# The triangle for the forget gates' running sums: one VectorE instruction per layer in the place of a load

## The chip, the core and the metric

The kernel runs on one core of a Trainium2 chip. The metric is device time in microseconds (us) of one execution of the program on that core; the figure for a kernel is the median of its runs. PE is TensorE (its weight loads have a row of their own, PEld), DVE is VectorE, ACT is ScalarE, POOL is GpSimd, SP is SyncE, whose queue issues all transfers of this kernel.

## What is computed

Two layers of a trunk over 1040 rows (16 learned rows and 1024 of input) of width 1024. In each layer the rows are normalized and projected; one half of the columns feeds four heads of differential attention, the other half eight heads of forgetting attention, whose scores carry a running sum of log forget gates. Gates, an output projection and the residual follow. What touches the change:

```python
    log_f = jax.nn.log_sigmoid(ff.astype(jnp.float32) + forget_bias[l].astype(jnp.float32))
    cum_logf = jnp.transpose(jnp.cumsum(log_f, axis=1), (0, 2, 1))
    ...
    # forgetting_attention, one block of queries
    s = jnp.einsum('bhqd,bhkd->bhqk', qb, k).astype(jnp.float32) * scale
    s = s + cq[..., None] - cum_logf[:, :, None, :]
    visible = positions[None, :] <= pq[:, None]
    s = jnp.where(visible, s, -jnp.inf)
```

## The kernel before

The 1040 rows are cut into nine blocks (80 rows, seven times 128, 64) and these into three chunks `c` of three blocks. Each layer is a weave of two streams, written by hand into one order for PE: the attention of eight pairs of heads (scores `sc`, transposes `tp`, products with the values `po`; all products are recorded at L181, transposes at L185), and the fill, which is the projections that the next pair needs (`k`, `q`, `v` and gate units; products `pj`). A model clock in the Python code decides at build time how the two are woven; PE then runs its list strictly in that order. On the other engines the order is set by a scheduler at build time, and each engine runs its list in order too.

The weights of a unit come as four loads of 128 KB into `wst` (four buffers, L254, on SP's queue) and are split into `whi` (ACT L261 or POOL L263) and `wlo` (POOL or DVE, L265).

The third value unit of a layer (`v_unit`, u = 2) also makes the eight columns of forget gates, collected in the tile `ffz` (called `z` in the code), 72 columns: nine blocks of eight heads. `log_forget` (L540 on) turns them into log forget gates by a chain on DVE with one exponential on ACT: L544, L546, L549 to L561. Its working tiles are three of the ring `tc`, which has three buffers in all. The last instruction, L561, writes `ffz`.

`cumulate` is a function that `log_forget` returns; it is called a little later in the stream. It takes a fourth tile `upper` from the ring `tc` (so the buffer of the first of the three working tiles, whose last reader is L559), loads the upper triangle of ones into it from the table `cst` in main memory (L566, 128 x 128 float32, 64 KB), and lets PE form the sums of each block over its rows, nine float32 products of the triangle with a block of `ffz` (18 instructions in the trace). L577 on DVE adds the sum of the block before, L579 writes the result to the scratch `cscr`, and L823 loads it from there for each head, spread over all partitions. The forgetting heads need it for their scores.

Two more tables lie on chip from the start of the program, in bfloat16, in one tile `cb16`: `identb`, the identity, and `trib`, 1e30 strictly above the diagonal and 0 elsewhere. The scores of the forgetting heads use both as a mask (L652). In the order of instructions below this tile is printed as `cb_67`; the `cb` without that number are tiles of the ring `cb`.

Of the kernel before, what the change touches and what calls it, by code (L numbers as in the profile page):

```python
# [13 lines left out]
ALU = mybir.AluOpType  # L14

P = 128
# [51 lines left out]
C_ID, C_U, C_DM, C_DM0 = 0, 128, 256, 256 + T  # L68
# [18 lines left out]
def trunk_kernel(ctx, tc, x, meta, norm_gain, w_in, fbias, lq1, lk1, lq2, lk2,  # L87
                 subln, w_out, fgain, cst, cstb, rope, out):
    nc = tc.nc
# [7 lines left out]
    dma = nc.sync.dma_start  # L97
# [4 lines left out]
    identb, trib = cb16[:, 0:P], cb16[:, P:2 * P]  # L102
# [25 lines left out]
    def st(tag, w, dt=F32, bufs=None):  # L128
        bufs = bufs or {"tc": TCB}.get(tag, 3)
        return sb.tile([P, w], dt, name=tag, tag=tag, bufs=bufs)  # L130

    def big(tag, bufs, dt=F32):
        return sb.tile([P, T], dt, name=tag, tag=tag, bufs=bufs)
# [45 lines left out]
    def mm(o, a, b, start, stop, passes=1):  # L179
        n = b.shape[-1]  # L180
        nc.tensor.matmul(o, a, b, start=start, stop=stop)  # L181
        pe.add(b.dtype == BF16, max(n * passes * COL, 0.056))
# [29 lines left out]
    def proj_ps(tag="pj"):  # L212
        return ps.tile([P, 512], F32, name=tag, tag=tag, bufs={"pj": 2, "sc": SB, "tp": TB}[tag])
# [326 lines left out]
    def log_forget(l, z, box):  # L540

        n = NB * 8
        az = st("tc", CW)[:, :n]
        nc.vector.scalar_tensor_tensor(az, z, -1.0, z, ALU.mult, ALU.max)  # L544
        e = st("tc", CW)[:, :n]
        nc.scalar.activation(e, az, AF.Exp, scale=-1.0)  # L546

        d = st("tc", CW)[:, :n]
        nc.vector.tensor_scalar(d, e, 2.0, None, ALU.add)  # L549
        nc.vector.reciprocal(d, d)  # L550
        s = az
        nc.vector.tensor_tensor(s, e, d, ALU.mult)
        w = d
        nc.vector.tensor_tensor(w, s, s, ALU.mult)
        q = e
        nc.vector.tensor_scalar(q, w, 1.0 / 15, None, ALU.mult)
        for i in (13, 11, 9, 7, 5, 3):
            nc.vector.scalar_tensor_tensor(q, q, 1.0 / i, w, ALU.add, ALU.mult)
        nc.vector.scalar_tensor_tensor(q, q, 1.0, s, ALU.add, ALU.mult)  # L559
        nc.vector.tensor_scalar(z, z, 0.0, None, ALU.min)  # L560
        nc.vector.scalar_tensor_tensor(z, q, -2.0, z, ALU.mult, ALU.add)  # L561

        def cumulate():
            crow = big("cb", 2)
            upper = st("tc", CW)
            dma(out=upper[:, 0:P], in_=cst[:, C_U:C_U + P])  # L566
            for c in range(3):
                pt = proj_ps("sc")
                for j in range(3 * c, 3 * c + 3):
                    sz = BE[j] - BS[j]  # L570
                    o = BS[j] - CS[c]
                    mm(pt[:8, o:o + sz], z[:sz, j * 8:(j + 1) * 8], upper[:sz, :sz], True, True, 4)
                for j in range(3 * c, 3 * c + 3):
                    o = BS[j] - CS[c]
                    sz = BE[j] - BS[j]
                    prev = crow[:8, BS[j] - 1:BS[j]] if j else zero1[:8, :]
                    nc.vector.tensor_scalar(crow[:8, BS[j]:BE[j]], pt[:8, o:o + sz], prev, None,  # L577
                                            ALU.add)
            dma(out=cscr[l], in_=crow[:8, :])  # L579
            box["cum"] = True  # L580
            when["cum"] = pe.t + LCUM
        return cumulate
# [631 lines left out]
```

## Time and profile before

| | |
|---|---|
| median of 3 runs | 1623.01 us |
| the runs | 1619.45 to 1624.98 us |
| the profiled execution, its own time | 1622.79 us |
| its span, first to last instruction | 1620.9 us |
| PE busy | 1486.1 us, 92% of the span |
| DVE busy | 1056.3 us, 65% |
| ACT busy | 829.6 us, 51% |
| POOL busy | 688.5 us, 42% |
| mean granted clock of PE | 0.964 |

Time stamps count from the first instruction of the profiled execution. "Busy" is the time in which an engine has an instruction under way; on PE matmuls overlap, so busy does not mean full speed. The granted clock is a share of 2.4 GHz: 1.00 is 2.4 GHz, 0.50 is 1.2 GHz. In a row of a timeline the brackets hold the idle time before the instruction and what ended it. A share of busy time is an average over stages; what a change in one place is worth is read from that place.

### The profile page before, as it was taken

What the parts mean: (1) busy time and instruction counts of PE and PEld (TensorE: products, weight loads), DVE (VectorE), ACT (ScalarE), POOL (GpSimd) and SP (SyncE); (2) the same over time, 40 slices, a digit from 0 to 9 for tenths busy, and PEclk for the clock granted to TensorE, in tenths of its full rate; (3) what the DMA queues carried; (4) which work ended last, traced back from release to release, by engine and by line L of the source; (5) the groups of instructions that cost most, each with busy time, mean ns of one, the idle gap of its engine ahead of it and who ended that gap; (6) DMA issues with size and microseconds to landing.
All of it is one profiled execution on the core that took longest, in us unless ns stands there. A gap on an engine that the chain in (4) does not pass through costs nothing.

```text
span 1620.9 us, 30144 instructions
## 1 busy us (share of the span) xinstructions
PE 1486.1 (92%) x9932; PEld 1419.7 (88%) x9932; DVE 1056.3 (65%) x3024; ACT 829.6 (51%) x2067; POOL 688.5 (42%) x1125
## 2 busy tenths in 40 slices
PE   6988999978999999987998999999599999996897
PEld 5988999977999999887988898999599999995897
DVE  6588867864756565666655986596556555657554
ACT  6455556533655565543334655565256555655543
POOL 3453423312444344456756243240244442443664
PEclk9999999998999999988999999999799999998999
DMA  9342313202232323464434242131222232334554
GB/s 240 86 100 60 97 46 63 60 19 71 69 68 63 103 58 99 151 184 133 146 78 104 62 96 73 33 75 28 64 58 67 58 93 57 92 114 143 151 148 137
DMA packets 181469, 147.86 MB, mean 91 GB/s; under 512 B 19624, under 2 KB 176864, under 8 KB 181312
## 3 DMA queue, kind: packets, MB, share of 16 engines
q1 hardware_dynamic: 181312, 145.93, 33.9%
q8 instruction: 79, 1.29, 0.3%
q14 instruction: 78, 0.64, 0.1%
HBM read 117.49 MB, written 28.38 MB: 90 GB/s over the span
## 4 chain that ended last, share of the span: by engine, by line
PE 57%; DVE 11%; DMA 8%; issue 6%; POOL 3%; ACT 2%; SPq 0%; DVEq 0%; POOLq 0%; ACTq 0%
PE pj L181 36%; PE sc L181 8%; PE po L181 7%; PE tp L185 6%; DMA wst<-in_w_out_dram 3%; DMA wst<-in_w_in_dram 2%; DVE wlo L265 2%; POOL wlo L265 1%; DVE e L656 1%; DMA oscr<-ta 1%; DMA actl<-oscr 1%; DVE actl L430 1%; DVE atl L748 1%; DMA tc<-in_cst_dram 1%; DVE kt L430 1%
## 5 line engine op out<-in xcount | busy, mean ns | idle before, releaser
L181 PE MATMUL pj<-acth,whi 128*128 128x320 f32 (+2 forms) x1536 | 519.5, 338 | 15.8 <-DVE hc L942 9.9
L181 PE MATMUL pj<-acth,wlo 128*128 128x320 f32 (+2 forms) x1536 | 498.6, 325 | 0.0
L181 PE MATMUL pj<-actl,whi 128*128 128x320 f32 (+2 forms) x1536 | 498.4, 324 | 0.0
L265 POOL TENSOR_TENSOR wlo<-wst,whi 128x256 fp32r<-128x256 f32 (+1 forms) x320 | 251.6, 795 | 185.4 <-ACT whi L261 140.1
L181 PEld LDWEIGHTS pj<-acth,whi 128*128 128x128 f32 x1536 | 296.9, 193 | 19.4 <-DVE hc L942 6.6
L181 PEld LDWEIGHTS pj<-acth,wlo 128*128 128x128 f32 x1536 | 296.0, 193 | 0.5
L181 PEld LDWEIGHTS pj<-actl,whi 128*128 128x128 f32 x1536 | 294.6, 192 | 0.4 <-DVE actl L430 0.4
L664 ACT ACTIVATE e<-e,mn 80x80 f32<-80x80 f32 (+8 forms) x288 | 225.7, 784 | 123.5 <-DVE mn L656 121.0
L748 DVE TENSOR_TENSOR atl<-tp,ath 128x320 fp32r<-128x320 f32 (+8 forms) x432 | 191.6, 449 | 81.8 <-ACT ath L747 77.6
L747 ACT ACTIVATE ath<-tp 128x320 fp32r<-128x320 f32 (+8 forms) x432 | 168.3, 404 | 128.3 <-PE tp L185 119.1
L261 ACT ACTIVATE whi<-wst 128x256 fp32r<-128x256 f32 (+1 forms) x304 | 124.6, 415 | 139.7 <-PE pj L181 53.0
L181 PE MATMUL sc<-kt,qq 128*128 128x296 f32 (+9 forms) x480 | 175.6, 368 | 15.8 <-DVE mn L656 11.5
L185 PE MATMUL tp<-ident,e 128*128 128x128 f32 (+2 forms) x1080 | 179.8, 274 | 0.7 <-POOL e L697 0.3
L697 POOL TENSOR_SCALAR e<-e,rl 80x80 f32<-80x80 f32 (+2 forms) x144 | 109.0, 758 | 161.6 <-DVE rl L696 151.1
L181 PE MATMUL po<-ath,v 128*128 128x256 f32 (+5 forms) x576 | 164.9, 327 | 10.1 <-ACT ath L747 10.1
L181 PE MATMUL pj<-whi,acth 128*128 128x256 f32 (+3 forms) x576 | 166.6, 289 | 4.1 <-DVE v L430 3.3
L181 PE MATMUL pj<-wlo,acth 128*128 128x256 f32 (+3 forms) x576 | 163.6, 284 | 2.8 <-POOL wlo L265 1.4
L181 PE MATMUL pj<-whi,actl 128*128 128x256 f32 (+3 forms) x576 | 163.1, 283 | 0.8 <-POOL actl L406 0.8
L181 PE MATMUL sc<-kt,ql 128*128 128x296 f32 (+9 forms) x480 | 158.2, 332 | 0.0
L181 PE MATMUL po<-atl,v 128*128 128x256 f32 (+5 forms) x432 | 137.3, 318 | 18.2 <-DVE atl L748 17.9
L185 PEld LDWEIGHTS tp<-ident,e 128*128 128x128 f32 (+2 forms) x1080 | 136.5, 139 | 6.5 <-POOL e L697 1.9
L265 DVE TENSOR_TENSOR wlo<-wst,whi 128x256 fp32r<-128x256 f32 (+1 forms) x128 | 88.5, 696 | 62.4 <-POOL whi L263 53.0
(166 smaller groups left out, 2483.5 us busy)
## 6 DMA issues: line engine op xcount, KB each, us to landing
wst<-in_w_in_dram SPq DMA_DIRECT2D x256, 128.0 KB
wst<-in_w_out_dram SPq DMA_DIRECT2D x192, 128.0 KB
cb<-cscr SPq DMA_DIRECT2D x16, 520.0 KB
cb<-in_rope_dram SPq DMA_DIRECT2D x20, 320.0 KB
cb<-in_rope_dram SPq DMA_DIRECT2D x16, 384.0 KB
oscr<-ta SPq DMA_DIRECT2D x26, 160.0 KB
cb<-in_rope_dram SPq DMA_DIRECT2D x12, 336.0 KB
oscr<-ta SPq DMA_DIRECT2D x20, 192.0 KB
```

The costliest lines, as they stand in the source:

```text
L181: nc.tensor.matmul(o, a, b, start=start, stop=stop)
L185: nc.tensor.transpose(o, a, idn)
L261: nc.scalar.activation(hi, sg_, AF.Copy)
L265: eng.tensor_tensor(lo, sg_, hi.bitcast(F32), ALU.subtract)
L430: nc.vector.tensor_tensor(lo, src, hi.bitcast(F32), ALU.subtract)
L656: nc.vector.tensor_tensor_reduce(e[rows, a:b], pt[rows, :b - a], bias(a, b)[rows, :], op0=ALU.add, op1=ALU.min, scale=1.0, scalar=least, a ...
L664: nc.scalar.activation(e[rows, :ext], e[rows, :ext], AF.Exp, scale=-1.0, bias=mn[rows, len(pcs) - 1:len(pcs)], accum_out=l[rows, :])
L697: nc.gpsimd.tensor_scalar(e[rows, :ext], e[rows, :ext], r[rows, 0:1], 1.0, ALU.mult, ALU.mult)
L747: nc.scalar.activation(ah[:kz, n0:w], tp[:kz, n0:w], AF.Copy)
L748: nc.vector.tensor_tensor(al[:kz, n0:w], tp[:kz, n0:w], ah[:kz, n0:w].bitcast(F32), ALU.subtract)
```

## The change

The load of the triangle is left out. In its place DVE makes the triangle from the two tables on chip: the smaller of `trib` and 1.0 is 1 strictly above the diagonal and 0 elsewhere, and adding the identity puts ones on the diagonal. `scalar_tensor_tensor` does both steps in one instruction, 128 x 128, bfloat16 in and float32 out.

```diff
         def cumulate():
             crow = big("cb", 2)
             upper = st("tc", CW)
-            dma(out=upper[:, 0:P], in_=cst[:, C_U:C_U + P])
+            nc.vector.scalar_tensor_tensor(upper[:, 0:P], trib, 1.0, identb, ALU.min, ALU.add)
             for c in range(3):
```

It moves a few instructions. PE, ACT and POOL keep their lists as they were. On DVE in layer 1, around the end of `log_forget` (`tc` are its working tiles and the triangle, `sc` the sums in PSUM, `cb` left of the arrow the running sums, `e` and `mn` the scores of the next block):

```order
 L558 SCALAR_TENSOR_TENSOR tc<-tc 128x72 x6
 L559 SCALAR_TENSOR_TENSOR tc<-tc 128x72
+L566 SCALAR_TENSOR_TENSOR tc<-cb_67 128x128
 L561 SCALAR_TENSOR_TENSOR ffz<-tc,ffz 128x72
 L577 TENSOR_SCALAR cb<-sc,zero_79 8x80
 L577 TENSOR_SCALAR cb<-sc,cb 8x128 x7
+L577 TENSOR_SCALAR cb<-sc,cb 8x64
 L660 TENSOR_SCALAR e,mn<-sc 128x488
-L577 TENSOR_SCALAR cb<-sc,cb 8x64
 L656 ISA e,mn<-sc,dm,mn 128x488
 L656 ISA mn 128x1
```

The new instruction stands between L559 and L561, so ahead of the last step of the chain, and the last of the nine L577 has moved ahead of one step of a score. In layer 0 only the new instruction is added, at the same place.

On SP in layer 1, behind the eight weight loads that are issued while the chain runs (`ta` and `oscr` are outputs of heads and their scratch):

```order
 L254 DMA wst<-in_w_in_dram 128x2x128 x8
-L566 DMA tc<-in_cst_dram 128x128
-L601 DMA ta<-oscr 128x336
 L579 DMA cscr<-cb 8x1040
-L790 DMA oscr<-ta 128x384
-L823 DMA cb<-cscr 128x1040 x2
+L601 DMA ta<-oscr 128x336
+L823 DMA cb<-cscr 128x1040
+L790 DMA oscr<-ta 128x384
+L823 DMA cb<-cscr 128x1040
 L601 DMA ta<-oscr 128x384
```

The load L566 is gone, and the load L601 of a head's output now stands behind the store L579, which waits for the running sums. In layer 0 the same load has gone and L601 and the first L823 have changed places behind L579.

## Rows read from the trace of the kernel before

**Rows 1.** PE's waits over the whole span: total us, times, longest us

```profile
PE sc L181 <- DMA tc<-in_cst_dram: 33.8, 2, 17.5
```

**Rows 2.** Timeline of PE, layer 0: start us, us, then the instruction

```profile
354.90 0.28 PE L181 MATMUL pj<-whi,actl 128*128 128x264 f32 x1
371.48 3.43 PE L181 MATMUL sc<-tc,ffz 80*8 80x80 f32 x18 [16.30 <-DMA tc<-in_cst_dram]
```

**Rows 3.** Timeline of DVE, layer 0, the chain's end

```profile
365.98 0.23 DVE L559 SCALAR_TENSOR_TENSOR tc<-tc 128x72 f32<-128x72 f32 x1
366.25 0.23 DVE L561 SCALAR_TENSOR_TENSOR ffz<-tc,ffz 128x72 f32<-128x72 f32 x1
```

**Rows 4.** Timeline of SP's queue, layer 0

```profile
354.58 9.57 SPq L254 DMA_DIRECT2D wst<-in_w_in_dram  x8
365.98 0.34 SPq L566 DMA_DIRECT2D tc<-in_cst_dram  x1
```

**Rows 5.** Timeline of PE, layer 1

```profile
1145.60 0.28 PE L181 MATMUL pj<-whi,actl 128*128 128x264 f32 x1
1163.41 3.41 PE L181 MATMUL sc<-tc,ffz 80*8 80x80 f32 x18 [17.53 <-DMA tc<-in_cst_dram]
```

**Rows 6.** Timeline of DVE, layer 1, the chain's end

```profile
1157.04 0.23 DVE L559 SCALAR_TENSOR_TENSOR tc<-tc 128x72 f32<-128x72 f32 x1
1157.30 0.23 DVE L561 SCALAR_TENSOR_TENSOR ffz<-tc,ffz 128x72 f32<-128x72 f32 x1
```

**Rows 7.** Timeline of SP's queue, layer 1

```profile
1157.03 0.34 SPq L566 DMA_DIRECT2D tc<-in_cst_dram  x1
1157.42 0.42 SPq L601 DMA_DIRECT2D ta<-oscr  x1
```

**Rows 8.** Busy time by stretch: stretch, length, PE, PEld, DVE, ACT, POOL, granted clock, DMA share, GB/s

```profile
364.20:371.00 6.80, 0.00 (x0) 0.00 (x0) 2.00 (x9) 0.00 (x0) 0.00 (x0) 0.50 0.34 63
371.00:371.45 0.45, 0.00 (x0) 0.00 (x0) 0.00 (x0) 0.00 (x0) 0.00 (x0) 0.50 0.00 0
1154.60:1163.10 8.50, 0.00 (x0) 0.00 (x0) 2.55 (x12) 0.00 (x0) 0.03 (x1) 0.50 0.55 69
```

**Rows 9.** Timeline of ACT, layer 0: the split of the first weight load

```profile
357.29 0.42 ACT L261 ACTIVATE whi<-wst 128x256 fp32r<-128x256 f32 x1 [1.80 <-DMA wst<-in_w_in_dram]
```

**Rows 10.** Timeline of DVE, layer 0: a 128 x 128 instruction of the new one's kind

```profile
352.31 0.29 DVE L432 SCALAR_TENSOR_TENSOR v<-pj,v 128x128 fp32r<-128x128 f32 x1
352.52 1.44 DVE L716 SCALAR_TENSOR_TENSOR e<-e,rl 128x1040 f32<-128x1040 f32 x1
...
380.91 0.50 DVE L432 SCALAR_TENSOR_TENSOR ql<-pj,qq 64x336 fp32r<-64x336 f32 x1 [0.22 <-ACT qq L428]
```

**Rows 11.** Timelines of DVE and PE: a result of DVE for which PE waits

```profile
703.70 0.48 DVE L748 TENSOR_TENSOR atl<-tp,ath 80x320 fp32r<-80x320 f32 x1
...
704.23 0.41 PE L181 MATMUL po<-atl,v 80*128 80x320 f32 x1 [1.02 <-DVE atl L748]
```

**Rows 12.** Busy time by stretch of 1 us: the granted clock around both waits

```profile
357.00:358.00 1.00, 0.00 (x0) 0.00 (x0) 0.00 (x0) 0.71 (x2) 0.22 (x1) 0.65 0.63 129
374.00:375.00 1.00, 1.00 (x8) 0.52 (x6) 0.85 (x3) 0.00 (x0) 0.00 (x0) 0.81 0.00 0
1149.00:1150.00 1.00, 0.00 (x0) 0.00 (x0) 0.20 (x1) 0.68 (x2) 0.39 (x1) 0.60 0.45 97
1166.00:1167.00 1.00, 1.00 (x8) 0.59 (x7) 0.92 (x3) 0.00 (x0) 0.00 (x0) 0.87 0.00 0
```

**Rows 13.** Timeline of PE and the granted clock after another wait

```profile
92.61 0.58 PE L181 MATMUL sc<-kt,qq 128*128 128x256 f32 x1 [3.77 <-DVE mn L656]
...
97.00:98.00 1.00, 1.00 (x6) 1.00 (x5) 1.00 (x6) 0.98 (x4) 0.00 (x0) 0.55 1.09 67
```

**Rows 14.** Busy time by stretch: PE behind the first wait, and two later falls of the clock

```profile
380.00:390.00 10.00, 10.00 (x70) 9.99 (x69) 4.97 (x13) 4.37 (x10) 2.89 (x6) 1.00 0.34 114
...
678.00:682.00 4.00, 3.59 (x15) 3.14 (x16) 2.32 (x8) 1.36 (x3) 2.20 (x3) 0.57 0.38 101
1538.00:1546.00 8.00, 5.40 (x23) 5.32 (x23) 5.90 (x18) 3.77 (x9) 3.89 (x7) 0.57 0.59 148
```

**Rows 15.** Timeline of POOL, layer 1: the first use of a `ta` that L601 loads

```profile
1190.30 0.88 POOL L623 TENSOR_TENSOR ta<-ta,tc 128x320 f32<-128x320 f32 x1 [0.18 <-POOL ql L475]
```

## The prediction

> **What bounds the kernel now.** The page gives PE 92% of the span, so the first view to read is PE's own waits. The longest group there is the wait of the first float32 sum for the triangle that L566 loads: 33.8 us in two waits [rows 1], one per layer. That is 2.1% of the span, and it would be a mistake to book all of it as a gain: the wait is put down to what came last, and the question is what comes second to last. So I read both places engine by engine.
>
> In layer 0 PE issues its last product of the value unit at 354.90 and then nothing until 371.48 [rows 2]. The same sums need two things: the triangle and the log forget gates in the tile ffz. The chain on DVE that makes ffz ends with L561, from 366.25 to 366.48 [rows 3]. The load of the triangle is issued only at 365.98 [rows 4], since its tile takes the buffer of the first working tile of that chain, whose last reader is L559 [rows 3]. So 11.3 of the 16.3 us are the chain, which stays, and 5.0 us lie behind it, from 366.48 to 371.48. In layer 1 it reads the same: L561 ends at 1157.53 [rows 6], the load is issued at 1157.03 [rows 7], PE starts at 1163.41 [rows 5], which leaves 5.9 us.
>
> That those 5.0 us belong to the load, and not to something the view doesn't show, is seen in the traffic: from 364.2 to 371.0 the queue moves 63 GB/s, and then until PE starts nothing [rows 8]. The load stands behind weight loads of 128 KB that were issued just before it (eight between 354.58 and 364.15 [rows 4]), and PE goes 0.5 us after the last byte has moved. In layer 1 the stretch before PE's start looks alike, 69 GB/s until 1163.1 [rows 8].
>
> **The change part by part.** *The load goes.* The sums no longer wait for a transfer. Two issues of 0.34 us on SP [rows 4, 7] go with it, which cost nothing either way: SP's next work behind them waits for the sums themselves.
>
> *One DVE instruction per layer comes,* and the order shows it between L559 and L561, so it delays the end of the chain by its length. The trace has no such instruction with bfloat16 in and float32 out. The nearest row is the same operation on 128 x 128 elements, L432: 0.29 us long, and the instruction behind it starts 0.21 us after it [rows 10]. Low end 0.21; high end 0.50, the same operation on 64 x 336 [rows 10]. I take 0.29, the row of the same shape. A gain is excluded: an instruction more in a chain can't shorten it.
>
> *The new start of PE.* A result of DVE reaches waiting PE within 0.05 us: L748 ends at 704.18, its product starts at 704.23 [rows 11]. Layer 0: 366.25 [rows 3] + 0.29 for the new instruction + 0.23 for L561 + 0.05 = 366.82, against 371.48 [rows 2]: 4.66 us. Layer 1: 1157.30 [rows 6] + 0.57 = 1157.87 against 1163.41 [rows 5]: 5.54 us. Sum 10.20 us; with 0.21 for the new instruction 10.36, with 0.50 it is 9.78.
>
> How a load is priced decides how much of this is believed. The rows say 5.2 us from the end of the issue (366.32 [rows 4]) to PE's start, and 6.0 us in layer 1 (1157.37 [rows 7]). The Trainium skill, "DMA: Bandwidth & Descriptors", section "Anatomy of one DMA" (on transfers that GpSimd issues; these go over SP's queue), fits about 2.0 us plus the bytes at 436 GB/s; for 64 KB that is an estimate of 2.15 us, so the triangle would land at 368.47 and 1159.52 and the sum would be 3.3 us and not 10.2. The rows show traffic up to 0.5 us before PE's start [rows 8], and the rows decide.
>
> *PE's clock.* It falls to 0.50 (1.2 GHz) during both waits, at 357.30 and 1149.20, some 2.1 and 3.3 us after PE's last product, and is back at 374.38 and 1166.26, so 2.9 us after PE's new start both times [rows 12], counted from the starts [rows 2, 5]. The shorter waits, 366.82 - 355.18 = 11.6 us and 12.0 us, are still far longer than what it took to fall, so the sums start at half clock as before. How long PE then works until the clock is back isn't fixed: after another wait it took from 92.61 to 97.90, 5.3 us [rows 13]. Work at half clock takes twice its time, so half of the added stretch is lost, and the bounds are 0 (2.9 us again) and 1.2 us per layer (5.3 us). I take 3.5 us, near the two rows of this place itself: 0.3 us per layer, 0.6 in all. That it comes back sooner than in the two rows I don't count on; it would gain at most 1.4 us per layer.
>
> *What moves with it.* SP's store L579 and the loads L823 of the running sums follow the sums and come earlier with them. In layer 1 the load L601 is moved behind L579, which waits for DVE: it goes out at about 1164 and not at 1157.42 [rows 7], and its first user starts at 1190.30 [rows 15], so some 20 us cover it even when that user comes 5.5 us earlier. On DVE the last L577 goes ahead of one step of a score (L660); what waits for that score also waits for the step behind it, L656, which comes after both in either order, so nothing changes. Behind the sums PE is busy 10.00 of 10 us [rows 14], at full clock, with no wait in which the gain could vanish: the weights of the next unit were loaded and split during the wait.
>
> **Sum.** 10.20 - 0.60 = 9.6 us less. The profiled execution took 1622.79 us, 1.9 us more than its span; it stands 0.2 us under the median of the runs, so no correction is due: 1622.79 - 9.60 = 1613.2 us.
>
> **The rivals.** *The load is not what PE waits for to the end.* Then part of the 5 us stays. The nearest price of a load in an emptier queue: the first weight load is issued at 354.58 [rows 4] and its split starts at 357.29 [rows 9], 2.71 us. A triangle that landed so would be there at 368.69 and 1159.74, the change would take away 1.87 us in each layer, and the time would be 1622.79 - 3.74 = 1619.0. Against it speaks the traffic that ends 0.5 us before PE starts [rows 8]; for it only that such waits are inferred. 6 in 100. This is the case in which the fit of "DMA: Bandwidth & Descriptors" in the Trainium skill would hold here, and by its 3.3 us the time would be 1619.5.
>
> *The gain is taken back downstream,* by a transfer that doesn't depend on PE and now comes late. I find none: the loads behind the sums are issued when PE or DVE free their buffers and move along. All 10 us lost would give 1623. 3 in 100.
>
> *Slower: the clock falls more often.* All that follows is shifted, by 4.7 us and then by 10.2, and whether a wait of some 3 us makes the clock fall depends on when it comes. Behind the first sums I count 11 falls besides the one in layer 1's wait and the one at the very end, from 678 to 1538 [rows 14]; a short one costs 4 us x (1 - 0.57) = 1.7 us. Six more eat the 9.6 us, and nine more end slower by over 0.3%, nearly twice the count of now. The waits themselves aren't changed, so falls will come and go in both directions; I expect two more or fewer. 3 in 100. The Trainium skill, "TensorE: Matmul & The Clock Gate", section on the clock gate, says that the monitor runs freely and does not restart with a kernel; nothing in this trace shows it.
>
> **How the numbers follow.** The forecast has 88 in 100. Its bounds: least gain 9.78 with 1.2 us per layer lost to the clock, 7.4, and one fall more, 1.7: 1617.1. Most gain 10.36 with no loss to the clock and two falls fewer, 3.4: 1609.0. That is the range; it leaves out the first two rivals, the slower one and the outer edge of the forecast, together about 2 in 10. About 0.3%, 4.9 us, can be told from no change in a measurement of this kernel: 1618.1 and below counts as faster. The forecast lies there, 0.88; the first two rivals give no change, 0.09; the third slower, 0.03.
>
> **What would show it.** In the changed kernel PE's waits list no load of a table at the sums; the first sum is released by L561 on DVE, about 11.6 and 12.0 us after the value unit's last product. The new instruction at L566 lasts 0.2 to 0.5 us and starts right behind L559. The granted clock is 0.50 when the sums start. PE's total of waits is some 10 us lower and its busy time within 1 or 2 us of now. I am wrong if PE's first sum starts more than 1 us after L561's end, if a wait that isn't there now appears within 30 us behind the sums, or if the busy time of PE behind them grows by over 3 us.

## The result and the profile after

| | before | after |
|---|---|---|
| median of 7 runs each | 1621.68 us | 1613.56 us |
| the runs | 1619.45 to 1625.96 | 1611.54 to 1617.85 |
| profiled execution, span | 1620.9 us | 1612.4 us |

The ratio is 0.9945, with a 95% interval from 0.9929 to 0.9960: faster by 0.55%, forecast 1613.2 us, measured 1613.56. (A ratio in this document need not be the quotient of the two medians, which is 0.9950 here.) That the times agree to within half a microsecond is luck. The gain was forecast as 9.6 us and came out at 8.1 by the medians and 8.5 by the two profiled executions; the sum set out from an execution of 1622.79 us, 1.1 us above the median of the seven runs, which hides most of the difference. The runs of one kernel lie some 6 us apart anyway.

First the view that the prediction started from, PE's waits over the whole span, of the changed kernel (total us, times, longest us):

```profile
PE sc L181 <- DVE ffz L561: 23.3, 2, 11.8
PE po L181 <- DVE atl L748: 19.2, 18, 3.1
PE sc L181 <- DVE mn L656: 11.2, 11, 3.8
```

Where the load of the table stood with 33.8 us [rows 1], the last step of the gates' chain stands now with 23.3. The wait is still the longest of the kernel; it has only lost its top. The same place in PE's timeline, layer 0 and layer 1:

```profile
356.91 0.28 PE L181 MATMUL pj<-whi,actl 128*128 128x264 f32 x1
368.64 3.73 PE L181 MATMUL sc<-tc,ffz 80*8 80x80 f32 x18 [11.45 <-DVE ffz L561]
...
1144.22 0.28 PE L181 MATMUL pj<-whi,actl 128*128 128x264 f32 x1
1156.35 3.73 PE L181 MATMUL sc<-tc,ffz 80*8 80x80 f32 x18 [11.85 <-DVE ffz L561]
```

16.30 and 17.53 us have become 11.45 and 11.85 [rows 2, 5]: 4.85 and 5.68 us less. What releases PE is read in DVE's timeline of the same place:

```profile
368.01 0.23 DVE L559 SCALAR_TENSOR_TENSOR tc<-tc 128x72 f32<-128x72 f32 x1
368.16 0.28 DVE L566 SCALAR_TENSOR_TENSOR tc<-cb 128x128 f32<-128x128 bf16 x1
368.36 0.22 DVE L561 SCALAR_TENSOR_TENSOR ffz<-tc,ffz 128x72 f32<-128x72 f32 x1
...
1155.71 0.23 DVE L559 SCALAR_TENSOR_TENSOR tc<-tc 128x72 f32<-128x72 f32 x1
1155.87 0.28 DVE L566 SCALAR_TENSOR_TENSOR tc<-cb 128x128 f32<-128x128 bf16 x1
1156.07 0.23 DVE L561 SCALAR_TENSOR_TENSOR ffz<-tc,ffz 128x72 f32<-128x72 f32 x1
```

L561 ends at 368.58 and PE starts at 368.64, 0.06 us later; in layer 1 it is 1156.30 and 1156.35. The new instruction lasts 0.28 us but costs less: it starts before L559 has ended, and L561 starts 0.20 us after it and not behind its end. From the start of L559 to that of L561 it is 0.35 us now and was 0.27 [rows 3], so the chain pays 0.08 us, and 0.10 in layer 1 (0.36 against 0.26 [rows 6]).

The whole difference is found by cutting both executions at these two waits. Busy time by stretch (stretch, length, PE, PEld, DVE, ACT, POOL, granted clock, DMA share, GB/s), first the kernel before, up to the first wait, between the two waits, behind the second:

```profile
0.00:355.18 355.18, 324.85 (x2165) 308.92 (x2165) 262.78 (x761) 193.50 (x486) 126.45 (x184) 0.99 0.35 86
371.48:1145.88 774.40, 733.33 (x4891) 702.71 (x4891) 510.25 (x1458) 392.67 (x989) 340.82 (x553) 0.97 0.33 88
1163.41:1620.90 457.49, 427.91 (x2876) 408.03 (x2876) 271.62 (x765) 237.31 (x576) 212.04 (x374) 0.97 0.36 102
```

and the changed kernel:

```profile
0.00:357.19 357.19, 326.26 (x2165) 310.35 (x2165) 263.40 (x761) 192.92 (x486) 126.74 (x184) 0.97 0.34 85
368.64:1144.50 775.86, 735.86 (x4891) 704.47 (x4891) 507.60 (x1458) 391.31 (x989) 342.28 (x553) 0.97 0.33 88
1156.35:1612.40 456.05, 428.16 (x2876) 407.85 (x2876) 271.27 (x765) 236.61 (x576) 211.13 (x374) 0.97 0.37 103
```

| us | before | after | difference |
|---|---|---|---|
| up to the first wait | 355.18 | 357.19 | +2.01 |
| first wait | 16.30 | 11.45 | -4.85 |
| between the waits | 774.40 | 775.86 | +1.46 |
| second wait | 17.53 | 11.85 | -5.68 |
| behind the second wait | 457.49 | 456.05 | -1.44 |
| span | 1620.90 | 1612.40 | -8.50 |

The two waits give 10.53 us. The other stretches give back 2.03 in all. The largest of them, +2.01, lies ahead of the first wait, where nothing of the change runs. There the clock differs. The first line is the kernel before, the second the changed one:

```profile
20.00:45.00 25.00, 20.02 (x120) 16.27 (x118) 20.95 (x53) 17.59 (x44) 9.78 (x11) 1.00 0.87 232
```

```profile
20.00:45.00 25.00, 20.13 (x110) 17.29 (x110) 22.51 (x55) 16.39 (x42) 10.71 (x12) 0.73 0.85 219
```

In the profiled execution of the changed kernel the clock fell in this stretch, to a mean of 0.73, and ten matmuls fewer started in it. It happened ahead of the change. In the profiles of the variants below, with the load and without it, the mean of the same stretch is anything from 0.73 to 1.00, so this goes from execution to execution and is not the change's.

### The profile page after: what moved, and what is told of

It reads as the page before. It is cut to its first block, busy times and chain, and to the rows that moved or that the text cites. A ratio compares the mean times of both kernels' runs of the same rounds, so it can differ in the third digit from the quotient of the medians.

```text
span 1612.4 us, 30136 instructions
## 1 busy us (share of the span) xinstructions
PE 1490.3 (92%) x9932; PEld 1422.7 (88%) x9932; DVE 1053.9 (65%) x3026; ACT 826.9 (51%) x2067; POOL 689.4 (43%) x1125
## 4 chain that ended last, share of the span: by engine, by line
PE 58%; DVE 10%; DMA 7%; issue 7%; POOL 4%; ACT 2%; SPq 0%; DVEq 0%; POOLq 0%; ACTq 0%
PE pj L181 37%; PE sc L181 8%; PE po L181 7%; PE tp L185 6%; DMA wst<-in_w_in_dram 2%; POOL wlo L265 2%; DMA wst<-in_w_out_dram 1%; DMA oscr<-ta 1%; DVE wlo L265 1%; DVE e L656 1%; DMA tc<-nscr 1%; DMA actl<-oscr 1%; DVE kt L430 1%; DVE atl L748 1%; DVE tc L422 1%
## 5 line engine op out<-in xcount | busy, mean ns | idle before, releaser
L181 PE MATMUL po<-atl,v 128*128 128x256 f32 (+5 forms) x432 | 137.7, 319 | 19.4 <-DVE atl L748 19.2
```

## The experiments

All variants below compute the same thing. Each is compared with runs of the kernel before on its own chip, whose medians were 1624.85 to 1625.70 us there, so ratios are compared and not times.

**A load that goes out early.** The kernel before with another tile for the triangle, one that is free at that time, so that the load does not wait for the ring:

```diff
-            upper = st("tc", CW)
+            upper = st("msr", P, bufs=1)
             dma(out=upper[:, 0:P], in_=cst[:, C_U:C_U + P])
```

> The kernel before, with the triangle still loaded, but into a tile of its own in the place of the fourth of the ring, so that the load can go out long before the chain of the gates. Theory (only the lateness of the load cost time, not that it was a load): PE's waits before the sums are released by the last step of the chain (L561), about 11.4 us in layer 0 and 11.8 us in layer 1 as in the changed kernel, and the time is the changed kernel's within 3 us (about 1613). Rival (the load's traffic among the weight loads costs the time, whenever it is issued, or PE waits for something else beside it): waits of 16.3 and 17.5 us stay in whole or in part, and the time is over 1617.

Measured: ratio 0.9943 (0.9918 to 0.9968), 1613.81 us, against 0.9945 of the changed kernel. The load goes out at 30.7 us for layer 0 and at 612.9 for layer 1, and PE's timeline reads:

```profile
371.34 3.73 PE L181 MATMUL sc<-msr,ffz 80*8 80x80 f32 x18 [11.06 <-DVE ffz L561]
...
1156.67 3.73 PE L181 MATMUL sc<-msr,ffz 80*8 80x80 f32 x18 [11.75 <-DVE ffz L561]
```

So the load was harmful by its time and not by its being a load: the same 64 KB, loaded without waiting for the ring's buffer, cost nothing that can be told, and the change's gain is had without the change. The theory holds and the rival falls. One thing stays open: in this profile PE reaches the first wait at 360.28 us, 3.1 us later than in the changed kernel. Whether the early load has a part in that is not shown.

**On chip in layer 0 alone.**

```diff
-            dma(out=upper[:, 0:P], in_=cst[:, C_U:C_U + P])
+            if l:
+                dma(out=upper[:, 0:P], in_=cst[:, C_U:C_U + P])
+            else:
+                nc.vector.scalar_tensor_tensor(upper[:, 0:P], trib, 1.0, identb, ALU.min, ALU.add)
```

> The triangle is made on chip in layer 0 and loaded in layer 1. Theory (each layer's wait is its own): a wait of about 11.4 us released by L561 in layer 0, one of about 17 us released by the load in layer 1, and the time about 4.5 us under the kernel before (1617). Rival (the gain is one layer's, the other is given back): the time of the changed kernel (1613) or of the one before (1622).

PE's waits (total us, times, longest us):

```profile
PE sc L181 <- DMA tc<-in_cst_dram: 17.4, 1, 17.4
...
PE sc L181 <- DVE ffz L561: 11.0, 1, 11.0
```

Both waits are as the theory has them, each for itself. The ratio is 0.9984 (0.9967 to 1.0002). The expected 4.5 us, a ratio of 0.9972, lie within that interval, but so does no gain at all: ten runs don't resolve a third of a per cent of this kernel, and the waits have to carry the verdict.

**The load on ScalarE's queue.**

```diff
-            dma(out=upper[:, 0:P], in_=cst[:, C_U:C_U + P])
+            nc.scalar.dma_start(out=upper[:, 0:P], in_=cst[:, C_U:C_U + P])
```

> The kernel before, with the load of the triangle issued on ScalarE's queue in the place of SP's, at the same moment (it still waits for its buffer, so for L559). Theory (the 5 to 6 us of the load are mostly weight loads that stand ahead of it in SP's queue): it lands about 2.7 us after its issue, as the first weight load of an empty queue did, so PE's waits are about 14 and 14.5 us and the time is some 5 us under the kernel before (1617). Rival (a load of this kind costs 5 us by itself, or shares the transfer engines with the weight loads whatever queue it is in): waits of 16 to 17.5 us and the time of the kernel before within 2 us.

Measured: ratio 1.0002 (0.9984 to 1.0020). The theory about the queue falls. In layer 0 the issue ends at 367.94 and PE starts at 373.07, 5.1 us later, as it was on SP's queue (5.2). In layer 1 it is 6.5 us, where it was 6.0; there the load L601 of a head's output is issued ahead of the triangle's now and was issued behind it before. First the issue, then PE, then the traffic by stretch:

```profile
367.56 0.38 ACTq L566 DMA_DIRECT2D tc<-in_cst_dram  x1
```

```profile
373.07 3.72 PE L181 MATMUL sc<-tc,ffz 80*8 80x80 f32 x18 [16.20 <-DMA tc<-in_cst_dram]
```

```profile
364.00:372.00 8.00, 0.00 (x0) 0.00 (x0) 3.65 (x13) 0.00 (x0) 1.34 (x2) 0.50 0.28 50
372.00:373.00 1.00, 0.00 (x0) 0.00 (x0) 0.00 (x0) 0.00 (x0) 0.00 (x0) 0.50 0.22 56
```

The traffic runs on until about half a microsecond before PE's start here too, at 50 to 56 GB/s where it was 63 [rows 8]. The Trainium skill, "DMA: Bandwidth & Descriptors", section "Issuing engines are not separate DMA queues", says that transfers which the scalar, sync or gpsimd engine issues run on the same 16 transfer engines and interleave, so that issuing on several engines only saves issue time; this run agrees with it. The other half of the rival, that such a load costs 5 us by itself, is excluded by a variant below, in which it took 2.6 us.

**The sums later in PE's order.** The wait that is left is the chain. Four variants put the sums behind other work of PE: the function that issues them is taken up by the fill stream once its model clock has passed a mark, and the mark is set 8 or 18 us behind the end of the chain's input.

```diff
-                box["lf"] = log_forget(l, z, box)
+                box["lf"], box["lft"] = log_forget(l, z, box), pe.t + 8.0
...
-            if u[0] in "vh":
+            if u[0] in "vh" and u != "v2":
```

For 18 us the first has 18.0. Both marks were built with the triangle made on chip and with the load. With the mark at 8:

> The changed kernel, with the sums put later into PE's order, behind about 9 us of projections and value products of the next unit that need nothing of the gates. Theory (the 11.4 and 11.8 us that are left of the two waits are the chain on DVE and ACT, which PE could have covered): waits before the sums of about 2.5 us each, no or short falls of the clock there, and a time about 20 us under the changed kernel (1593). Rival (the engines beside PE need that pause to catch up, so PE waits elsewhere): the waits turn up at other lines within 30 us and the time falls by less than 8 us.

> The kernel before, with the load, and the sums put equally late, behind about 9 us of other work of PE. Theory (the load's 5 us lie behind the chain, whatever PE does meanwhile): waits of about 7.5 and 8.5 us released by the load, and a time about 10 us over its twin with the triangle made on chip. Rival (the load is hidden as soon as PE has other work): the same time as the twin within 3 us.

and at 18:

> The changed kernel with the sums still later, behind about 17.5 us of other work of PE. Theory: no wait before the sums, no fall of the clock there, a time of about 1588 if nothing behind waits for the running sums, and up to 5 us more if the first scores of the forgetting heads do. Rival (those scores become the wait): over 1600.

> The kernel before, with the load, and the sums behind about 17.5 us of other work of PE, which is longer than chain and load together (16.3 and 17.5 us). Theory (the change is worth what the load sticks out behind PE's other work): no wait of over 1 us for the load, and the time of its twin with the triangle made on chip within 2 us, so the change is worth nothing here. Rival (making the triangle on chip saves time by itself): about 10 us over the twin.

The first measurement (four runs each) left the comparison of the twins open, so the same four kernels were measured again on another chip, with four to six runs each:

> A second measurement, with more rounds and all four variants on one chip: triangle made on chip, sums behind about 9 us of other work of PE. Theory (a load costs what it sticks out behind chain and other work; in the profiles of the first measurement the waits before the sums add up to 10.3 us here and 16.8 us in the twin): about 5 us under its twin with the load. Rival (no difference, as the medians of 1607 and 1609 may also be read): within 2 us of the twin.

> The twin with the load, sums behind about 9 us of other work. Theory: about 5 us over the twin with the triangle made on chip. Rival: within 2 us of it.

> Triangle made on chip, sums behind about 17.5 us of other work of PE, so that the profile has no wait before them. Theory (the change is worth nothing where the load is covered): within 2 us of its twin with the load, both about 1.4% under the kernel before. Rival (the instruction on DVE costs or saves by itself): 4 us or more apart, as the medians of 1606 and 1601 of the first measurement would say if taken at their word.

> The twin with the load, sums behind about 17.5 us of other work. Theory: within 2 us of the twin with the triangle made on chip. Rival: 4 us or more under it.

| sums behind | triangle | first ratio (95%) | second ratio (95%) | second median |
|---|---|---|---|---|
| mark 8 | on chip | 0.9886 (0.9860 to 0.9912) | 0.9864 (0.9842 to 0.9885) | 1603.32 us |
| mark 8 | load | 0.9902 (0.9877 to 0.9928) | 0.9905 (0.9886 to 0.9925) | 1610.08 us |
| mark 18 | on chip | 0.9875 (0.9849 to 0.9902) | 0.9844 (0.9818 to 0.9869) | 1599.54 us |
| mark 18 | load | 0.9852 (0.9828 to 0.9875) | 0.9861 (0.9838 to 0.9885) | 1601.92 us |

At mark 18 the change is worth nothing that can be told: the twins' medians are 5.9 us apart in the one measurement and 2.4 us in the other, with opposite signs. A difference of some 2 us either way stays open; the second measurement's 2.4 us lie between the theory's 2 and the rival's 4. In the profiles neither waits before its sums for the load or for the chain, and the sums run at full clock. The matmuls that read the gates (count: shortest, median and longest in ns, then first and last start in us), first of the changed kernel, then of the variant with mark 18 and the triangle on chip (second measurement, as all that follows on mark 18):

```profile
L181 PE MATMUL sc<-tc,ffz x36: 273/417/421, 368.6 to 1159.8; 128*8 128x128 f32 x28, 80*8 80x80 f32 x4, 64*8 64x64 f32 x4
```

```profile
L181 PE MATMUL sc<-tc,ffz x36: 215/272/274, 377.8 to 1165.0; 128*8 128x128 f32 x28, 80*8 80x80 f32 x4, 64*8 64x64 f32 x4
```

Both waits are gone, 23.3 us, and yet the profiled execution is only 13.5 us shorter than that of the changed kernel. About half of the gain comes back as other waits of PE (total us, times, longest us):

```profile
PE po L181 <- DVE atl L748: 23.1, 20, 3.2
PE po L181 <- DVE ta L786: 3.9, 2, 2.7
```

In the changed kernel the first was 19.2 and the second did not occur. PE's idle time as a whole fell from 122.1 us (span 1612.4, busy 1490.3) to 110.3 (1598.9, 1488.6). The rival's mechanism is there too: in layer 0 the first forgetting scores wait 2.7 us for the running sums, on DVE (L656 for the load into `cb`). But in the 45 us behind the sums PE loses only 1.5 us in layer 0 and 1.1 us in layer 1, so this is not the main part of what kept mark 18 from the expected 1588. The waits that grew stand late in the layers: from 600 to 720 us those for `atl` are 11.7 us, where they were 4.0. That the work which was put ahead of the sums is missing there is likely and not shown.

At mark 8 the change is worth 6.8 us by the second measurement, where about 5 were expected, and 2.5 by the first. The intervals of the twins overlap in the first and just miss each other in the second. The profiles show why it isn't 10. PE's waits before the sums, first with the triangle on chip, then with the load (first measurement):

```profile
PE sc L181 <- DVE ffz L561: 10.3, 2, 5.4
```

```profile
PE sc L181 <- DMA tc<-in_cst_dram: 16.8, 2, 9.1
```

With the load it is 7.7 and 9.1 us, as expected. On chip it is 5.4 and 4.8, twice what was expected, because the chain isn't 11.4 us long when PE goes on working. DVE, mark 8, on chip, layer 0:

```profile
366.52 0.16 DVE L713 RECIPROCAL rl<-ls 128x1 f32<-128x1 f32 x1 [1.96 <-ACT e L664]
366.71 0.54 DVE L714 SCALAR_TENSOR_TENSOR rl<-rl,neglam,l 128x1 f32<-128x1 f32 x1
367.18 0.18 DVE L549 TENSOR_SCALAR tc<-tc 128x72 f32<-128x72 f32 x1
367.29 1.24 DVE L716 SCALAR_TENSOR_TENSOR e<-e,rl 128x976 f32<-128x976 f32 x1
...
369.08 0.50 DVE L432 SCALAR_TENSOR_TENSOR ql<-pj,qq 64x336 fp32r<-64x336 f32 x1
...
372.75 0.23 DVE L561 SCALAR_TENSOR_TENSOR ffz<-tc,ffz 128x72 f32<-128x72 f32 x1
```

Scores and projections that PE has gone on to produce (L713 to L716, L432) stand between the steps of the chain, and L561 ends 14.3 us after the value unit's last product (358.69 in this run) and no longer 11.4. In the twin it is 13.9. The load had less to wait for: PE starts 2.6 us after the end of its issue in layer 0, and 4.1 us in layer 1. SP's queue and PE of the twin, layer 0 and layer 1:

```profile
365.73 0.38 SPq L254 DMA_DIRECT2D wst<-in_w_in_dram  x1
370.09 0.34 SPq L566 DMA_DIRECT2D tc<-in_cst_dram  x1
...
1147.16 0.38 SPq L254 DMA_DIRECT2D wst<-in_w_in_dram  x1
1151.97 0.34 SPq L566 DMA_DIRECT2D tc<-in_cst_dram  x1
```

```profile
373.02 3.71 PE L181 MATMUL sc<-tc,ffz 80*8 80x80 f32 x18 [7.68 <-DMA tc<-in_cst_dram]
...
1156.39 3.72 PE L181 MATMUL sc<-tc,ffz 80*8 80x80 f32 x18 [9.08 <-DMA tc<-in_cst_dram]
```

The last weight load is issued 4.4 us before the triangle's in layer 0 and 4.8 us in layer 1, so its age alone doesn't set the price. In both layers, as in the kernel before, traffic runs until 0.1 to 0.7 us before PE starts. Behind L561 the load sticks out by 2.4 and 3.9 us here (5.0 and 5.9 in the kernel before), 6.3 in all, and 5.9 in the second measurement's profile. That is near its 6.8 us and well under 10.

So both halves of my expectation of 10 us were off: a chain without neighbours and a load among its neighbours were priced, and here it was the other way round. The expectation of 1593 and 1588 us was also too good: mark 8 came to 1607 and 1603, mark 18 to 1606 and 1600. Still, the two kernels with mark 18 are the fastest here, 1.25 to 1.56% under the kernel before by the four ratios, where the change alone gives 0.55. Which of the twins is the faster is not told: with the load it was so in the first measurement, on chip in the second.

## Why the prediction was right

**The bound and what comes second.** It was read from the place and not from the total: of 33.8 us booked on the load, 10.53 were its own in the profile. The chain, which the prediction said stays, is what PE waits for now: it starts 0.05 to 0.06 us after L561's end, in both layers. One step of the argument was weaker than it was put: in layer 1 the load L601 is issued 0.4 us behind the triangle's [rows 7], so the traffic up to PE's start could not show there that the wait was the triangle's, and SP's next work did not wait for the sums. What settles it is the early load.

**The terms.** Start of PE: 4.66 and 5.54 us were forecast, 4.85 and 5.68 measured. Nearly all of the 0.19 and 0.14 us more comes from the new instruction, which was priced at its full length of 0.29 us: it is 0.28 us long, but only 0.08 to 0.10 us of it delay L561. The low end, 0.21, was not low enough, since the overlap with the instruction ahead was left out.

**The clock.** It had fallen when the sums began, as forecast, and came back later than the 3.5 us that I took. The changed kernel by stretches of 1 us, around the first and the second return:

```profile
373.00:374.00 1.00, 1.00 (x6) 0.87 (x6) 0.63 (x3) 0.00 (x0) 0.00 (x0) 0.94 0.00 0
...
1161.00:1162.00 1.00, 1.00 (x5) 0.82 (x4) 0.34 (x2) 0.00 (x0) 0.00 (x0) 0.70 0.14 24
```

A mean of 0.94 means half clock for 0.12 us, so it returned at 373.12, 4.5 us after PE's start, and in layer 1 at 1161.60, 5.2 us after. Against 2.9 us before, half of the added stretch is 0.8 and 1.2 us, 2.0 in all where 0.6 was forecast. Both lie within the bounds that the row of another wait had set (5.3 us). PE's timeline gives a little less: the first product of the next projection (`pj<-acth,whi`) starts 5.72 and 6.07 us after the first sum, and started 5.06 and 5.05 us after it before, so 1.7 us are lost. That half clock takes twice the time is a little too much: the eighteen sums of a layer take 3.73 us at half clock and 2.04 at full clock, in the profile of the variant with mark 18. So the waits gained 0.3 us more than forecast and the clock took 1.1 us more; both are of the size of what changes from run to run anyway.

**Downstream.** PE is busy 10.00 of 10 us behind the sums, as before, and nothing took the gain back there. L601, which moved behind L579 in layer 1, is issued at 1161.55, and its first user starts at 1184.27: over 20 us of cover, as said. PE's busy time rose by 4.2 us in all, more than the 1 to 2 us named, of which 1.4 us lie ahead of the first wait and 2.8 behind, just under the 3 us that I had set as a sign of error.

**The rivals.** That PE waits for something else beside the load is excluded by the early load, which ends the wait at L561 without a change on DVE. The 2.15 us per load of the Trainium skill's fit ("DMA: Bandwidth & Descriptors", "Anatomy of one DMA") were not what the load cost here; the nearest to it were 2.6 and 2.3 us, in layer 0 of the two measurements of mark 8 with the load. The clock's falls behind the first sums, not counting the one in layer 1's wait and the one at the very end, are 11 in the changed kernel (from 676 to 1533) as they were 11 before, so the slower rival had nothing to work with.

## What to carry to other kernels

When the profile names the last of several releasers, look up when the others were done: the gain of removing the last one ends at the second, here 5 of 16 us. A small constant that is loaded late costs by its lateness; how much varied from 2.3 to 6.5 us here, probably with the traffic around it, which no run varied alone. Another buffer for it, free earlier, was worth as much as making it on chip. And a wait of PE for a chain on other engines may be a matter of where its consumer stands in PE's own order: moving it gave more than the change, though less than the wait was long. At mark 8 the chain shares DVE with the work that fills the gap; at mark 18 the wait is gone and other waits of PE grow.

## What the runs showed that I had not expected

- The same 64 KB took 5.2 and 6.0 us (layer 0 and layer 1) from the end of its issue to PE's start with weight loads issued shortly before it, 5.1 and 6.5 on another queue, and 2.6 and 4.1 us when the last weight load was 4.4 and 4.8 us old.
- Neighbouring instructions of DVE of which none reads what the one ahead writes overlap here: the triangle's starts 0.15 us after the start of L559, which lasts 0.23, and L561 starts 0.20 us after it though it lasts 0.28.
- How much work at half clock follows a wait of some 11 to 17 us varied from 2.9 to 5.2 us at this one place, which alone moved the time by 0.7 and 1.0 us in the two layers.
- A fall of the clock in the first 45 us, in the profiled execution of the changed kernel and not in that of the kernel before, went with 2.0 us of difference ahead of anything that the change touches.
